# A two-layer decoder on one core: transposes moved ahead in each attention unit, maxima ahead of exponentials, probabilities scaled on ScalarE, every second low part of the weights made on GpSimd

## The chip, the cores and the metric

The kernel runs on one core of one Trainium2 chip, as one launch. The metric is the device time of that launch in microseconds (us). The kernel before took 1246.62 us as the median of three runs (1243.71 to 1250.85). The execution that the profile shows took 1248.97 us.

## The reference

Layer 1 is a RetNet layer (4 heads, chunks of 128) with a gate, an output projection and a gated embedding. Layer 2 is sparse attention with 16 heads in 4 groups over keys and values that the group shares. Everything is float32, 512 tokens by 1024.

```python
proj = rmsnorm(h, g_norm) @ w_in                     # layer 2
q, gate, bgate = jnp.split(proj, [q_w, q_w + NSA_W], axis=-1)
# per block of 128 queries:
p_c = softmax over the 31 compressed keys            # masked, causal
o_c = p_c @ v_cmp
idx = top_k(score, min(16, number of blocks))        # blocks of 64 keys
p_s = softmax over the keys of the selected blocks   # masked, causal
p_w = softmax over the last 512 keys                 # masked, causal
return gates[..., 0:1] * o_c + gates[..., 1:2] * o_s + gates[..., 2:3] * o_w
y = (silu(gate) * o) @ w_out
```

With 512 tokens there are 8 blocks, so all of them are selected, and the window of 512 reaches back to the first token. Both are plain causal attention, each with keys and values of its own. The compressed branch has 32 columns.

## The kernel before

**Arithmetic.** Every product is made from three: each operand is split into a high part (fp32r, a ScalarE copy) and a low part (the rest, a VectorE subtraction), and TensorE multiplies high by high, high by low and low by high (`mm3`). So each 128x512 result costs three passes for each 128 rows of depth.

**Weights.** `Stream` brings the weights in, 176 pieces of 128x1024 floats in a fixed order, through 4 raw buffers and 6 slots for the two parts. `mul` (line 176) multiplies a piece by its gain on GpSimd in two halves, `high` (line 190) copies it on ScalarE, `low` (line 205) subtracts on VectorE, and then `load` issues the DMA of a later piece into the raw buffer that became free (line 143, SP's queue). `tick(2)` does low, high, mul twice.

**The attention loop.** It goes through 4 groups `g` and in each through 8 units `u`: 4 heads, and of each the selected branch (`u` even, compressed columns with it) and the window branch (`u` odd). An iteration makes the scores of the next unit and the values of the current one, with projections in between that are independent (`fill(0)`, `fill(1)`, `fill(2)`; `PLAN` and `PARTS` say how many steps of 12 matmuls each has). In order:

- `scores(next)`: 15 matmuls into three banks tagged `s`; on VectorE the masks and the maxima (line 953), on ScalarE the exponentials into `P` (line 954). For the first two blocks of queries, which share a bank, a maximum and its exponential alternate. The compressed scores are added to their mask afterwards (line 893).
- `fill(0)`, then `scale_probs`: VectorE inverts the sums (962, 963), GpSimd multiplies `P` by them in four pieces (966).
- `fill(1)`, then `probs_split`: ScalarE copies the current unit's transposed probabilities `pt2` to `tH` (985), VectorE makes `tL` (986).
- `probs_T` for the next unit: VectorE transposes 32x32 blocks of `P` into `pt1` (975), four DMAs write them to DRAM (979), one brings them back in the other order into `pt2` (982).
- `W.tick(2)`, the sums of the compressed branch (900 to 903, and 904 on GpSimd), `cmp_T`, `fill(2)`, and `values(current)`: 12 matmuls from `tH` and `tL` into a bank tagged `o`.

The program runs in the order in which it is written, on each engine for itself; SP's queue as well issues its DMAs in that order and waits at each for what it needs. PSUM has eight banks: two `d`, three `s`, two `pt`, one `o`. Results of the projections in the loop go to `d`: a query or gate projection is two steps and one bank; a step of the output projection (`pair_tiles`) is two banks, and each is added to `hacc` on VectorE (1021). After the last unit of a group come the value projections of the next, and before it the key projections (`k_proj`), so the iterations u = 6 and 7 are long.

Of the kernel before, what the change touches and what calls it, by code (L numbers as in the profile page):

```python
# [11 lines left out]
F32 = mybir.dt.float32  # L12
# [3 lines left out]
OP = mybir.AluOpType  # L16
# [101 lines left out]
class Stream:  # L118
# [75 lines left out]
                self.nc.scalar.activation(hi[:, c], raw[:, c], AF.Copy, scale=g[:, k:k + 1])  # L194
        self.nh += 1

    def low(self):
        n = self.ns
        if n >= self.nh:
            return  # L200
        s = self.place[n]
        raw, m, w, g = self.parts(n)
        hi, lo = self.hi[s].bitcast(F32), self.lo[s]
        if g is None or w < 512:
            self.nc.vector.tensor_sub(lo[:, :m * w], raw, hi[:, :m * w])  # L205
        else:
            for k in range(m):
                c = slice(k * w, k * w + w)
                self.nc.vector.scalar_tensor_tensor(lo[:, c], raw[:, c], g[:, k:k + 1], hi[:, c],  # L209
                                                    op0=OP.mult, op1=OP.subtract)  # L210
        self.ns += 1
        self.load()
# [24 lines left out]
def decoder(ctx: ExitStack, tc: tile.TileContext, x, xT, stream, cst, msk, gains, fnorm, out):  # L237
# [32 lines left out]
    bg = V(fb + 508, 192).rearrange("p (t c) -> p t c", t=NT)  # L270
    fb += 700

    def psum(tag, shape=None):
        n = {"d": 2, "s": 3, "pt": 2, "o": 1}[tag]
        return ps.tile([128, 512], F32, name=tag, bufs=n)

# [198 lines left out]
    def run(g):  # L475
        for _ in g:
            pass
# [257 lines left out]

    def q_proj(g, h):
        p = W.get("nin", 0, 1024, 512 * g + 128 * h, 128)
        o = psum("d")
        wst(p, o, 0, 4)
        yield  # L740
        wst(p, o, 4, 8)
        s = 128 ** -0.5
        act.activation(q2H[h], o, AF.Copy, scale=s)
        dve.scalar_tensor_tensor(q2L[h], o, s, q2H[h].bitcast(F32), op0=OP.mult, op1=OP.subtract)
        W.tick()
        p.done()
        yield

    def g_proj(g, h):
        p = W.get("nin", 0, 1024, 2048 + 512 * g + 128 * h, 128)  # L750
        o = psum("d")
        wst(p, o, 0, 4)
        yield
        wst(p, o, 4, 8)
        x = g2[h % 2]
        act.activation(x, o, AF.Tanh, scale=0.5)
        dve.scalar_tensor_tensor(x, x, 1.0, o, op0=OP.add, op1=OP.mult)
        W.tick()
        p.done()
        yield  # L760
# [125 lines left out]
    PO = [0, 384, 768, 1152]  # L886
    JB = [0, 128, 224, 288]

    def cmp_probs(g, h, banks):

        q, q4 = pc[h % 2], pc4[h % 2]
        for i, o in banks:
            dve.tensor_add(q[:, i:i + 2], o, cmask[:, i:i + 2])
        mx, sm_ = scal(4), scal(4)
        dve.reduce_max(mx, q, axis=mybir.AxisListType.X)
        dve.tensor_sub(q, q, mx[:, :, None].to_broadcast([128, 4, 32]))
        yield
        act.activation(q, q, AF.Exp)
        yield
        dve.reduce_sum(sm_, q, axis=mybir.AxisListType.X)  # L900
        dve.reciprocal(sm_, sm_)
        dve.tensor_mul(sm_, sm_, bg[:, :, 12 * g + 3 * h])
        dve.tensor_mul(sm_, sm_, rowv)
        pool.tensor_mul(q4, q[:, :, None, :].to_broadcast([128, 4, 3, 32]),
                        sm_[:, :, None, None].to_broadcast([128, 4, 3, 32]))
        yield
# [11 lines left out]
    def scores(g, u):  # L918
        h, b = divmod(u, 2)
        e = 0 if b else 32  # L920
        mx, sm_ = scal(4), scal(4)
        cmp = []

        def block(w, i, lo, hi):
            c = slice(128 * i, 128 * i + 128)
            mm3(w, [(q2H[h][:, c], q2L[h][:, c], k2H[b][:, lo:hi], k2L[b][:, lo:hi])], True, True)

        for bank in ((3,), (2,), (0, 1)):
            o = psum("s")
            f, at = 0, []  # L930
            for i in bank:
                lo = e if i == 3 else 0
                n = 128 * i + 128 + e - lo
                block(o[:, f:f + n], i, lo, lo + n)
                at.append(f + e - lo)
                f += n
            if e and 2 in bank:
                block(o[:, 416:448], 3, 0, 32)
                cmp.append((2, o[:, 0:448].rearrange("p (a n) -> p a n", a=14)[:, 0:14:13]))
            elif e and 0 in bank:  # L940
                cmp.append((0, o[:, 0:480].rearrange("p (a n) -> p a n", a=3)[:, 0:2, :32]))
            if 1 in bank:

                d = bass.AP(tensor=o.tensor, offset=o.offset + e,
                            ap=[list(o.ap[0]), [256 + e, 2], [1, 128]])
                dve.tensor_add(d, d, tri[:, None, :].to_broadcast([128, 2, 128]))
            else:
                d = o[:, at[0] + 128 * bank[0]:][:, :128]
                dve.tensor_add(d, d, tri)
            for i, f in zip(bank, at):  # L950
                n = 128 * i + 128
                w = o[:, f:f + n]
                dve.reduce_max(mx[:, i:i + 1], w, axis=mybir.AxisListType.X, negate=True)  # L953
                act.activation(P[:, PO[i]:PO[i] + n], w, AF.Exp, bias=mx[:, i:i + 1],  # L954
                               accum_out=sm_[:, i:i + 1])
        chain = cmp_probs(g, h, cmp) if e else iter(())
        next(chain, 0)
        return sm_, chain

    def scale_probs(g, u, sm_):  # L960
        h, b = divmod(u, 2)
        dve.reciprocal(sm_, sm_)
        dve.tensor_mul(sm_, sm_, bg[:, :, 12 * g + 3 * h + b + 1])
        for i in (3, 2, 0, 1):
            w = P[:, PO[i]:PO[i] + 128 * i + 128]
            pool.tensor_scalar(w, w, sm_[:, i:i + 1], 1.0, op0=OP.mult, op1=OP.mult)  # L966

    def view(a, o, *ap):
        return bass.AP(tensor=a.tensor, offset=a.offset + o, ap=[list(a.ap[0])] + [list(d) for d in ap])

    def probs_T():


        for j in range(NT):
            dve.transpose(view(pt1, JB[j], (32, NT - j), (320, 4), (1, 32)),  # L975
                          view(P, PO[j] + 128 * j, (384, NT - j), (32, 4), (1, 32)))
        m = dr.tile([128, 1280], F32, name="moved")
        for a in range(4):
            nc.sync.dma_start(bass.AP(tensor=m.tensor, offset=m.offset + 320 * a,
                                      ap=[[1280, 32], [32 * 1280, 4], [1, 320]]),  # L980
                              pt1[32 * a:32 * a + 32].rearrange("p (b n) -> p b n", b=4))
        nc.sync.dma_start(pt2, m)

    def probs_split():
        act.activation(tH, pt2, AF.Copy)  # L985
        dve.tensor_sub(tL, pt2, tH.bitcast(F32))  # L986

    def values(g, u, o):
# [24 lines left out]
                yield  # L1013

    def pair_tile(c, t, p):
        o = psum("d")
        s = slice(128 * t, 128 * t + 128)
        mm3(o, [(y2H[:, k, s], y2L[:, k, s], p.h[:, k], p.l[:, k])
                for k in range(2)], True, True)
        d = hacc[:, t, 512 * c:512 * c + 512]  # L1020
        dve.tensor_add(d, d, o)  # L1021
# [10 lines left out]
    next(comp1)  # L1032
    w2p.done()
    probs_T()
    run(chain)
    k_proj(0, 1)

# [3 lines left out]
    for g in range(GROUPS):  # L1041
        f = fillers(g)
        for u in range(8):
            h = u // 2
            last = (g, u) == (3, 7)
            W.auto = False
            left = 2 * len(between(g, h))
            first = 4 if h == 3 else left // 2
            n = PLAN[u] if g == 3 else left - first if u % 2 else first
            steps = [1, 1, 0] if last else PARTS[n]  # L1050

            def fill(i):
                for _ in range(steps[i]):
                    next(f)

            sums = None
            if u < 7:
                nxt = g, u + 1
            elif g < 3:
                k_proj(g + 1, 0)  # L1060
                k_proj(g + 1, 1)
                nxt = g + 1, 0
            else:
                nxt = None
            if nxt:
                sums, chain = scores(*nxt)
            fill(0)
            if sums is not None:
                scale_probs(*nxt, sums)
            next(chain, 0)  # L1070
            fill(1)
            probs_split()
            if sums is not None:
                probs_T()
            W.tick(0 if last else 2)
            next(chain, 0)
            if u % 2 == 0:
                cmp_T(h)
            fill(2)
            if u % 2 == 0:  # L1080
                o_head = psum("o")
            values(g, u, o_head)
            W.auto = True
        run(f)
        if g < 3:
            p = v_pieces(g + 1)
            for t in range(NT):
                v_proj(g + 1, t, p, ("d", "pt")[t % 2], t % 2)
# [101 lines left out]
```

## Time and profile before

| what | before |
|---|---|
| time of the profiled execution | 1248.97 us |
| its span, first to last instruction | 1247.2 us |
| TensorE matmuls busy | 1146.7 us (92%) |
| VectorE busy | 753.4 us (60%) |
| ScalarE busy | 485.5 us (39%) |
| GpSimd busy | 324.9 us (26%) |
| mean granted TensorE clock | 0.96 |

The shares are means over stages that differ. Up to 586 us TensorE hardly stops; the attention loop from there to about 1180 us is where it waits. Matmuls are pipelined, so their busy time is not a measure of their speed. The granted clock is 1.00 at 2.4 GHz and 0.50 at 1.2 GHz; a mean between says how the stretch is shared between the two.

### The profile page before, as it was taken

The numbers are of one execution on the slowest core, as the hardware profiler recorded it, in microseconds if no ns is written. First come the engines' busy times: TensorE is split into PE (matmuls) and PEld (weight loads), VectorE is DVE, ScalarE is ACT, GpSimd is POOL, SyncE is SP. The second block draws the span as 40 slices with busy tenths as digits, with TensorE's granted clock in tenths as the row PEclk, the third lists the DMA queues.
The fourth block names the chain that finished last, engine by engine and source line by source line (L and its number), as shares of the span: only waits on it lengthen the run. The fifth ranks groups of instructions, "written<-read, shape, count | busy, mean of one in ns | idle before, by whom it ended". The sixth has DMA issues, their size and how long they took to land. (4 is left out here: it accounts for less than half of the span.)

```text
span 1247.2 us, 14924 instructions
## 1 busy us (share of the span) xinstructions
PE 1146.7 (92%) x5486; PEld 961.9 (77%) x5486; DVE 753.4 (60%) x1290; ACT 485.5 (39%) x852; POOL 324.9 (26%) x357
## 2 busy tenths in 40 slices
PE   9999999999999999997878898879988799878797
PEld 7888888888888888886767787768877688666686
DVE  4745446346435565566666656776576766777455
ACT  6432233233234554464333334442344323443454
POOL 0121012003002123556242304243134422221102
PEclk9999999999999999999788999999999899979899
DMA  8422322322322313454343333443424443353311
GB/s 326 138 73 85 105 85 85 101 93 68 105 81 68 115 39 124 155 161 135 99 150 119 110 118 115 152 135 106 138 83 146 135 135 110 107 170 124 99 51 68
DMA packets 52633, 143.84 MB, mean 115 GB/s; under 512 B 6096, under 2 KB 22736, under 8 KB 52560
## 3 DMA queue, kind: packets, MB, share of 16 engines
q1 hardware_dynamic: 52128, 142.10, 35.4%
q8 instruction: 43, 0.70, 0.2%
q10 hardware_dynamic: 432, 0.79, 0.2%
q14 instruction: 30, 0.25, 0.1%
HBM read 119.80 MB, written 23.07 MB: 115 GB/s over the span
## 5 line engine op out<-in xcount | busy, mean ns | idle before, releaser
L356 PE MATMUL d<-arenaR 128*128 128x512 f32 (+2 forms) x2904 | 686.2, 391 | 39.7 <-DVE arenaF L1021 27.2
L356 PEld LDWEIGHTS d<-arenaR 128*128 128x128 f32 x2904 | 538.4, 193 | 152.9 <-DVE arenaF L1021 32.3
L356 PE MATMUL s<-arenaR 128*128 128x512 f32 (+8 forms) x1182 | 249.1, 363 | 3.4 <-ACT arenaF L954 1.8
L356 PEld LDWEIGHTS s<-arenaR 128*128 128x128 f32 x1182 | 208.6, 197 | 35.1 <-ACT arenaF L954 2.0
L205 DVE TENSOR_TENSOR arenaR<-arenaF,arenaR 128x1024 fp32r<-128x1024 f32 (+1 forms) x142 | 179.6, 1282 | 67.0 <-ACT arenaR L190 66.8
L190 ACT ACTIVATE arenaR<-arenaF 128x1024 fp32r<-128x1024 f32 (+1 forms) x142 | 145.9, 1046 | 120.4 <-PE s L356 68.4
L356 PE MATMUL o<-arenaR 128*128 128x512 f32 (+3 forms) x744 | 148.5, 351 | 42.3 <-ACT arenaR L985 21.9
L356 PEld LDWEIGHTS o<-arenaR 128*128 128x128 f32 x744 | 126.3, 209 | 65.2 <-ACT arenaR L985 25.9
L176 POOL TENSOR_TENSOR arenaF<-arenaF 128x512 f32<-128x512 f32 x108 | 126.2, 1190 | 154.8 <-DMA arenaF<-stream_dram 150.4
L966 POOL TENSOR_SCALAR arenaF<-arenaF 128x512 f32<-128x512 f32 (+3 forms) x128 | 84.5, 678 | 231.2 <-ACT arenaR L985 79.8
L954 ACT ACTIVATE arenaF<-s,arenaF 128x512 f32<-128x512 f32 (+3 forms) x128 | 67.6, 528 | 134.4 <-DVE arenaF L953 132.3
L372 POOL TENSOR_TENSOR arenaF<-arenaF 128x1 f32<-128x1 f32 (+1 forms) x25 | 14.2, 568 | 292.3 <-DVE arenaF L371 292.3
L953 DVE TENSOR_REDUCE arenaF<-s 128x1 f32<-128x512 f32 (+3 forms) x128 | 62.8, 491 | 22.9 <-ACT arenaF L954 19.6
L356 PE MATMUL pt<-arenaR 128*128 128x512 f32 (+1 forms) x384 | 75.9, 349 | 0.0
L975 DVE STREAM_TRANSPOSE arenaF<-arenaF 128x512 f32<-128x512 f32 (+3 forms) x128 | 57.7, 489 | 25.0 <-POOL arenaF L966 23.9
L356 PEld LDWEIGHTS pt<-arenaR 128*128 128x128 f32 x384 | 62.8, 189 | 9.4
L209 DVE SCALAR_TENSOR_TENSOR arenaR<-arenaF,arenaR 128x512 fp32r<-128x512 f32 x64 | 45.7, 762 | 35.0 <-PE pt L356 21.4
L986 DVE TENSOR_TENSOR arenaR<-arenaF,arenaR 128x1280 fp32r<-128x1280 f32 x32 | 50.4, 1575 | 19.6 <-ACT arenaR L985 19.6
L194 ACT ACTIVATE arenaR<-arenaF 128x512 fp32r<-128x512 f32 x64 | 43.1, 720 | 46.5 <-issue 22.3
L1000 ACT ACTIVATE arenaR<-arenaF 128x512 fp32r<-128x512 f32 x16 | 10.1, 633 | 130.0 <-DVE arenaF L999 130.0
L1021 DVE TENSOR_TENSOR arenaF<-arenaF,d 128x512 f32<-128x512 f32 x64 | 42.0, 682 | 25.1 <-PE d L356 24.8
L985 ACT ACTIVATE arenaR<-arenaF 128x1280 fp32r<-128x1280 f32 x32 | 40.6, 1267 | 2.8 <-DMA arenaF<-moved 2.7
(125 smaller groups left out, 741.5 us busy)
## 6 DMA issues: line engine op xcount, KB each, us to landing
arenaF<-stream_dram SPq DMA_DIRECT2D x174, 512.0 KB, 4.2
moved<-arenaF SPq DMA_DIRECT2D x128, 160.0 KB, 2.8
arenaF<-moved SPq DMA_DIRECT2D x32, 640.0 KB, 4.0
arenaF<-xT_dram SPq DMA_DIRECT2D x8, 256.0 KB, 4.8
arenaF<-x_dram SPq DMA_DIRECT2D x4, 512.0 KB, 7.6
out_dram<-arenaF SPq DMA_DIRECT2D x3, 512.0 KB, 2.7
arenaF<-cst_dram SPq DMA_DIRECT2D x4, 256.0 KB, 3.9
arenaF<-stream_dram ACTq DMA_DIRECT2D x2, 256.0 KB, 3.4
```

What stands on the lines that cost most here:

```text
L176: self.nc.gpsimd.tensor_mul(r3[:, k], r3[:, k], g[:, k, None].to_broadcast([128, m // 2, w]))
L190: self.nc.scalar.activation(hi[:, :m * w], raw, AF.Copy)
L194: self.nc.scalar.activation(hi[:, c], raw[:, c], AF.Copy, scale=g[:, k:k + 1])
L205: self.nc.vector.tensor_sub(lo[:, :m * w], raw, hi[:, :m * w])
L209: self.nc.vector.scalar_tensor_tensor(lo[:, c], raw[:, c], g[:, k:k + 1], hi[:, c], op0=OP.mult, op1=OP.subtract)
L356: pe.matmul(o, a, b, start=start and i == 0, stop=stop and i == n - 1)
L953: dve.reduce_max(mx[:, i:i + 1], w, axis=mybir.AxisListType.X, negate=True)
L954: act.activation(P[:, PO[i]:PO[i] + n], w, AF.Exp, bias=mx[:, i:i + 1], accum_out=sm_[:, i:i + 1])
L966: pool.tensor_scalar(w, w, sm_[:, i:i + 1], 1.0, op0=OP.mult, op1=OP.mult)
L975: dve.transpose(view(pt1, JB[j], (32, NT - j), (320, 4), (1, 32)), view(P, PO[j] + 128 * j, (384, NT - j), (32, 4), (1, 32)))
L986: dve.tensor_sub(tL, pt2, tH.bitcast(F32))
L1021: dve.tensor_add(d, d, o)
```

## The change

Inside an iteration the current unit's split goes to the front, in two halves around the scaling; the scaling goes to ScalarE; the next unit's transposes and their four outgoing DMAs go ahead of `fill(1)`; the DMA back is issued just ahead of `values`. The weights' two rounds of low, high, mul are spread over the iteration, and the second low is made on GpSimd. Projections take a bank by the tag `f`, that is `d`, `pt`, `d` in turn.

```diff
-    def low(self):
+    def low(self, engine=None):
-            self.nc.vector.tensor_sub(lo[:, :m * w], raw, hi[:, :m * w])
+            (engine or self.nc.vector).tensor_sub(lo[:, :m * w], raw, hi[:, :m * w])
...
+    turn = [0]
     def psum(tag, shape=None):
+        if tag == "f":
+            turn[0] += 1
+            tag = ("d", "d", "pt")[turn[0] % 3]
...
-        o = psum("d")          # q_proj, g_proj, pair_tile
+        o = psum("f")
...
             for i, f in zip(bank, at):
+                dve.reduce_max(mx[:, i:i + 1], o[:, f:f + 128 * i + 128],
+                               axis=mybir.AxisListType.X, negate=True)
+            if cmp:
+                i, d = cmp
+                dve.tensor_add(pc[h % 2][:, i:i + 2], d, cmask[:, i:i + 2])
+            for i, f in zip(bank, at):
                 n = 128 * i + 128
-                w = o[:, f:f + n]
-                dve.reduce_max(mx[:, i:i + 1], w, axis=mybir.AxisListType.X, negate=True)
-                act.activation(P[:, PO[i]:PO[i] + n], w, AF.Exp, bias=mx[:, i:i + 1],
+                act.activation(P[:, PO[i]:PO[i] + n], o[:, f:f + n], AF.Exp, bias=mx[:, i:i + 1],
                                accum_out=sm_[:, i:i + 1])
...
-        for i in (3, 2, 0, 1):
+        for i in (3, 2, 1, 0):
             w = P[:, PO[i]:PO[i] + 128 * i + 128]
-            pool.tensor_scalar(w, w, sm_[:, i:i + 1], 1.0, op0=OP.mult, op1=OP.mult)
+            act.activation(w, w, AF.Copy, scale=sm_[:, i:i + 1])
...
     def probs_T():
-        for j in range(NT):
+        for j in (3, 2, 1, 0):
...
-        nc.sync.dma_start(pt2, m)
-    def probs_split():
+    def probs_back():
+        nc.sync.dma_start(pt2, moved.pop(0))
+    def probs_high():
         act.activation(tH, pt2, AF.Copy)
+    def probs_low():
         dve.tensor_sub(tL, pt2, tH.bitcast(F32))
...
                 sums, chain = scores(*nxt)
+            W.low()
             fill(0)
+            probs_high()
             if sums is not None:
                 scale_probs(*nxt, sums)
+            probs_low()
             next(chain, 0)
-            fill(1)
-            probs_split()
+            W.high()
+            W.mul()
             if sums is not None:
                 probs_T()
-            W.tick(0 if last else 2)
+            fill(1)
             next(chain, 0)
+            if not last:
+                W.low(nc.gpsimd)
+                W.high()
+                W.mul()
             if u % 2 == 0:
                 cmp_T(h)
             fill(2)
+            if sums is not None:
+                probs_back()
```

VectorE in iteration g = 1, u = 1, from the additions of `fill(0)` on, before: 1021 are additions to `hacc`, 962 and 963 invert the sums, 986 is `tL`, 975 the transposes, 205 the low parts, 900 to 903 the compressed sums.

```order
L1021 TENSOR_TENSOR arenaF<-arenaF,d 128x512 x2
L962 RECIPROCAL arenaF<-arenaF 128x4
L963 TENSOR_TENSOR arenaF<-arenaF 128x4
L1021 TENSOR_TENSOR arenaF<-arenaF,d 128x512 x2
L986 TENSOR_TENSOR arenaR<-arenaF,arenaR 128x1280
L975 STREAM_TRANSPOSE arenaF<-arenaF 128x4x4x32
L975 STREAM_TRANSPOSE arenaF<-arenaF 128x3x4x32
L975 STREAM_TRANSPOSE arenaF<-arenaF 128x2x4x32
L975 STREAM_TRANSPOSE arenaF<-arenaF 128x4x32
L205 TENSOR_TENSOR arenaR<-arenaF,arenaR 128x1024 x2
L900 TENSOR_REDUCE arenaF<-arenaF 128x4
```

The same place of the change (1035 are the additions, 970 and 971 invert the sums, 1000 is `tL`, 985 the transposes):

```order
L205 TENSOR_TENSOR arenaR<-arenaF,arenaR 128x1024
L1035 TENSOR_TENSOR arenaF<-arenaF,d 128x512 x2
L970 RECIPROCAL arenaF<-arenaF 128x4
L971 TENSOR_TENSOR arenaF<-arenaF 128x4
L1000 TENSOR_TENSOR arenaR<-arenaF,arenaR 128x1280
L985 STREAM_TRANSPOSE arenaF<-arenaF 128x4x32
L985 STREAM_TRANSPOSE arenaF<-arenaF 128x2x4x32
L985 STREAM_TRANSPOSE arenaF<-arenaF 128x3x4x32
L985 STREAM_TRANSPOSE arenaF<-arenaF 128x4x4x32
L1035 TENSOR_TENSOR arenaF<-arenaF,pt 128x512
L1035 TENSOR_TENSOR arenaF<-arenaF,d 128x512
L903 TENSOR_REDUCE arenaF<-arenaF 128x4
```

`tL` and the transposes now stand ahead of the additions of `fill(1)`; one low part stands ahead of the additions of `fill(0)`, and the other has left VectorE.

SP's queue in the iterations g = 1, u = 0 and 1, before (979 writes the transposed blocks, 982 brings them back, 143 loads weights):

```order
L979 DMA moved<-arenaF 32x4x320 x4
L982 DMA arenaF<-moved 128x1280
L143 DMA arenaF<-stream_dram 128x1024
L979 DMA moved<-arenaF 32x4x320 x4
L982 DMA arenaF<-moved 128x1280
L143 DMA arenaF<-stream_dram 128x1024 x2
```

The same iterations in the change (989 writes, 994 brings back):

```order
L989 DMA moved<-arenaF 32x4x320 x4
L143 DMA arenaF<-stream_dram 128x1024
L994 DMA arenaF<-moved 128x1280
L143 DMA arenaF<-stream_dram 128x1024
L989 DMA moved<-arenaF 32x4x320 x4
L143 DMA arenaF<-stream_dram 128x1024
L994 DMA arenaF<-moved 128x1280
```

A load that waits for a low part on GpSimd now stands between the writes and the DMA that brings them back.

ScalarE in iteration g = 1, u = 1, before (954 the exponentials, 898 that of the compressed branch, 985 `tH`, 190 high parts):

```order
L954 ACTIVATE arenaF<-s,arenaF 128x512
L954 ACTIVATE arenaF<-s,arenaF 128x384
L954 ACTIVATE arenaF<-s,arenaF 128x128
L954 ACTIVATE arenaF<-s,arenaF 128x256
L898 ACTIVATE arenaF<-arenaF 128x128
L985 ACTIVATE arenaR<-arenaF 128x1280
L190 ACTIVATE arenaR<-arenaF 128x1024 x2
```

And of the change (962 the exponentials, 997 `tH`, 974 the scaling, 901 the compressed branch):

```order
L962 ACTIVATE arenaF<-s,arenaF 128x512
L962 ACTIVATE arenaF<-s,arenaF 128x384
L962 ACTIVATE arenaF<-s,arenaF 128x128
L962 ACTIVATE arenaF<-s,arenaF 128x256
L997 ACTIVATE arenaR<-arenaF 128x1280
L974 ACTIVATE arenaF<-arenaF 128x512
L974 ACTIVATE arenaF<-arenaF 128x384
L974 ACTIVATE arenaF<-arenaF 128x256
L974 ACTIVATE arenaF<-arenaF 128x128
L901 ACTIVATE arenaF<-arenaF 128x128
L190 ACTIVATE arenaR<-arenaF 128x1024 x2
```

`tH` stays behind the exponentials, and the four scalings stand behind it.

## Rows read from the trace of the kernel before

**Rows 1.** Windows: bounds, length, busy us per engine (instructions), PEclk, DMA share, GB/s

```profile
0.00:586.50 586.50, 577.33 (x2759) 484.16 (x2759) 317.63 (x436) 229.16 (x340) 134.13 (x123) 1.00 0.34 114
603.70:699.10 95.40, 79.58 (x337) 65.87 (x338) 67.02 (x133) 36.86 (x76) 31.75 (x40) 0.86 0.40 126
749.80:849.60 99.80, 83.82 (x387) 69.22 (x387) 71.70 (x142) 39.15 (x80) 40.54 (x48) 0.93 0.39 121
902.90:1002.30 99.40, 84.33 (x387) 69.72 (x386) 72.84 (x143) 39.02 (x80) 41.16 (x47) 0.91 0.38 119
1002.30:1053.80 51.50, 48.36 (x275) 42.12 (x274) 30.27 (x60) 17.59 (x34) 10.18 (x14) 1.00 0.41 126
1053.80:1146.20 92.40, 74.93 (x339) 61.09 (x338) 68.52 (x139) 36.51 (x76) 23.94 (x33) 0.91 0.41 129
1146.20:1197.20 51.00, 43.67 (x200) 35.90 (x199) 29.69 (x54) 24.90 (x45) 6.18 (x8) 0.93 0.39 124
```

**Rows 2.** Windows of two single iterations, columns as in Rows 1

```profile
762.80:781.80 19.00, 14.90 (x67) 12.17 (x66) 14.40 (x30) 5.83 (x12) 2.92 (x5) 0.91 0.33 98
800.00:812.60 12.60, 12.60 (x66) 10.86 (x65) 7.65 (x17) 6.09 (x13) 2.81 (x4) 1.00 0.59 180
```

**Rows 3.** TensorE's waits: who for whom, us in total, times, longest us

```profile
PE d L356 <- DVE arenaF L1021: 27.2, 16, 3.4
PE o L356 <- ACT arenaR L985: 21.9, 11, 3.0
PE o L356 <- DVE arenaR L986: 13.2, 12, 1.6
PE d L356 <- DVE arenaF L757: 11.9, 4, 4.8
PE pt L912 <- POOL arenaF L904: 6.2, 2, 3.1
```

**Rows 4.** Timeline 1109 to 1124 us: start, us, instruction, idle before and its end

```profile
1109.15 1.27 ACT L985 ACTIVATE arenaR<-arenaF 128x1280 fp32r<-128x1280 f32 x1
1110.45 1.50 DVE L986 TENSOR_TENSOR arenaR<-arenaF,arenaR 128x1280 fp32r<-128x1280 f32 x1 [1.42 <-ACT arenaR L985]
1112.59 1.84 DVE L975 STREAM_TRANSPOSE arenaF<-arenaF 128x512 f32<-128x512 f32 x4 [0.64 <-POOL arenaF L966]
1114.46 1.88 SPq L979 DMA_DIRECT2D moved<-arenaF  x4
1115.46 0.27 DVE L900 TENSOR_REDUCE arenaF<-arenaF 128x4 f32<-128x128 f32 x1
...
1116.52 0.83 POOL L904 TENSOR_TENSOR arenaF<-arenaF 128x384 f32<-128x384 f32 x1 [3.96 <-DVE arenaF L903]
...
1118.84 0.34 SPq L982 DMA_DIRECT2D arenaF<-moved  x1
...
1123.12 1.27 ACT L985 ACTIVATE arenaR<-arenaF 128x1280 fp32r<-128x1280 f32 x1 [0.21 <-DMA arenaF<-moved]
```

**Rows 5.** Groups by line: xcount, busy us, mean ns of one, idle before and releasers

```profile
L966 POOL TENSOR_SCALAR arenaF<-arenaF 128x512 f32<-128x512 f32 (+3 forms) x128 | 84.5, 678 | 231.2 <-ACT arenaR L985 79.8 <-ACT arenaF L898 67.5 <-DVE arenaF L963 43.7
L954 ACT ACTIVATE arenaF<-s,arenaF 128x512 f32<-128x512 f32 (+3 forms) x128 | 67.6, 528 | 134.4 <-DVE arenaF L953 132.3 <-PE s L356 0.6 <-PE d L356 0.3
L953 DVE TENSOR_REDUCE arenaF<-s 128x1 f32<-128x512 f32 (+3 forms) x128 | 62.8, 491 | 22.9 <-ACT arenaF L954 19.6
L1021 DVE TENSOR_TENSOR arenaF<-arenaF,d 128x512 f32<-128x512 f32 x64 | 42.0, 682 | 25.1 <-PE d L356 24.8
```

**Rows 6.** Single lines: xcount, shortest, median and longest ns, first and last start

```profile
L176 POOL TENSOR_TENSOR arenaF<-arenaF x108: 1030/1040/2289, 439.8 to 1067.9; 128x512 f32<-128x512 f32 x108
L205 DVE TENSOR_TENSOR arenaR<-arenaF,arenaR x142: 679/1218/2062, 14.3 to 1160.2; 128x1024 fp32r<-128x1024 f32 x138, 128x912 fp32r<-128x912 f32 x2, 128x608 fp32r<-128x608 f32 x1, 128x512 fp32r<-128x512 f32 x1
L428 POOL TENSOR_TENSOR arenaF<-arenaF x8: 1278/1289/2200, 35.7 to 307.7; 128x512 f32<-128x512 f32 x8
```

**Rows 7.** DMA issues: xcount, KB each, median us from issue to landing

```profile
arenaF<-stream_dram SPq DMA_DIRECT2D x174, 512.0 KB, 4.2
```

More of the change, by code (lines that the diff above doesn't have):

```diff
@@ L750, in g_proj @@
         p = W.get("nin", 0, 1024, 2048 + 512 * g + 128 * h, 128)
-        o = psum("d")
+        o = psum("f")
         wst(p, o, 0, 4)
@@ L887, in decoder, with cmp_probs @@
     JB = [0, 128, 224, 288]
-    def cmp_probs(g, h, banks):
+    def cmp_probs(g, h):
         q, q4 = pc[h % 2], pc4[h % 2]
-        for i, o in banks:
-            dve.tensor_add(q[:, i:i + 2], o, cmask[:, i:i + 2])
         mx, sm_ = scal(4), scal(4)
@@ L921, in scores @@
         mx, sm_ = scal(4), scal(4)
-        cmp = []
         def block(w, i, lo, hi):
@@ L938, in scores @@
                 block(o[:, 416:448], 3, 0, 32)
-                cmp.append((2, o[:, 0:448].rearrange("p (a n) -> p a n", a=14)[:, 0:14:13]))
+                cmp = 2, o[:, 0:448].rearrange("p (a n) -> p a n", a=14)[:, 0:14:13]
             elif e and 0 in bank:
-                cmp.append((0, o[:, 0:480].rearrange("p (a n) -> p a n", a=3)[:, 0:2, :32]))
+                cmp = 0, o[:, 0:480].rearrange("p (a n) -> p a n", a=3)[:, 0:2, :32]
+            else:
+                cmp = None
             if 1 in bank:
@@ L950, in scores @@
             for i, f in zip(bank, at):
+                dve.reduce_max(mx[:, i:i + 1], o[:, f:f + 128 * i + 128],
[4 more added lines that the diff above has]
+            for i, f in zip(bank, at):
                 n = 128 * i + 128
-                w = o[:, f:f + n]
-                dve.reduce_max(mx[:, i:i + 1], w, axis=mybir.AxisListType.X, negate=True)
-                act.activation(P[:, PO[i]:PO[i] + n], w, AF.Exp, bias=mx[:, i:i + 1],
+                act.activation(P[:, PO[i]:PO[i] + n], o[:, f:f + n], AF.Exp, bias=mx[:, i:i + 1],
                                accum_out=sm_[:, i:i + 1])
-        chain = cmp_probs(g, h, cmp) if e else iter(())
+        chain = cmp_probs(g, h) if e else iter(())
         next(chain, 0)
@@ L963, in scale_probs @@
         dve.tensor_mul(sm_, sm_, bg[:, :, 12 * g + 3 * h + b + 1])
-        for i in (3, 2, 0, 1):
+        for i in (3, 2, 1, 0):
             w = P[:, PO[i]:PO[i] + 128 * i + 128]
-            pool.tensor_scalar(w, w, sm_[:, i:i + 1], 1.0, op0=OP.mult, op1=OP.mult)
+            act.activation(w, w, AF.Copy, scale=sm_[:, i:i + 1])
     def view(a, o, *ap):
         return bass.AP(tensor=a.tensor, offset=a.offset + o, ap=[list(a.ap[0])] + [list(d) for d in ap])
+    moved = {}
     def probs_T():
-        for j in range(NT):
+        for j in (3, 2, 1, 0):
             dve.transpose(view(pt1, JB[j], (32, NT - j), (320, 4), (1, 32)),
                           view(P, PO[j] + 128 * j, (384, NT - j), (32, 4), (1, 32)))
-        m = dr.tile([128, 1280], F32, name="moved")
+        m = moved[0] = dr.tile([128, 1280], F32, name="moved")
         for a in range(4):
@@ L1015, in pair_tile @@
     def pair_tile(c, t, p):
-        o = psum("d")
+        o = psum("f")
         s = slice(128 * t, 128 * t + 128)
@@ L1079, in decoder @@
             fill(2)
+            if sums is not None:
+                probs_back()
             if u % 2 == 0:
```

## The prediction

> **What bounds the kernel now.** I read the windows first. Up to 586.5 us TensorE is busy for 577.3 of 586.5 us at a clock of 1.00 [rows 1]: nothing is to be had there, and the change hardly touches it. In the attention loop each of the four stretches of six short units (603.7 to 699.1, 749.8 to 849.6, 902.9 to 1002.3, 1053.8 to 1146.2) has TensorE idle for 15 to 17 us, at a clock of 0.86 to 0.93, so part of it is at 1.2 GHz [rows 1]. Two iterations with the same matmuls show the size: one without a wait takes 12.6 us at clock 1.00, one with waits 19.0 us at 0.91 [rows 2]. No engine is full: VectorE has 67 to 73 us in 92 to 100.
>
> The waits, read second, have three kinds [rows 3]: for a `d` bank that VectorE has not added or gated yet (1021, 757: 39.1 us), for `tH` and `tL` in `values` (985, 986: 35.1 us), for the compressed probabilities from GpSimd (904: 6.2 us). They are waits for order rather than for work. `tH` stands on ScalarE behind the evacuation of `fill(1)`, and the additions stand on VectorE behind the whole softmax.
>
> Third, the timeline of one unit shows the loop underneath [rows 4]: `tH` at 1109.15 (1.27), `tL` at 1110.45 (1.50), transposes at 1112.59 (1.84), first write at 1114.46, the way back issued at 1118.84, next `tH` at 1123.12, released by that DMA. That is 13.97 us from `tH` to `tH`; without the 0.64 that the transposes wait for GpSimd's scaling it is 13.3. Each link follows from the one before, in the changed order too: `tL` precedes the next transposes on VectorE, and the next `tH` needs their DMA. So 13.3 us is a floor for a unit, above the 12.6 us that TensorE needs for the longest of the short ones, and against (95.4 + 99.8 + 99.4 + 92.4) / 24 = 16.1 us that they take.
>
> **The change part by part.** *Split ahead of `fill(1)`.* `tH` now waits for the exponentials and its DMA alone. The 35.1 us go as far as the floor allows; what is late next is the round trip.
>
> *Bank tag `f`.* Three or four results can be open instead of two. In a unit with six output tiles TensorE then stops perhaps once, for a tile whose addition stands behind the maxima and one low part; I cost that at nothing, since the floor covers it. The 39.1 us go. If that cover fails it is the second rival.
>
> *Scaling on ScalarE.* GpSimd loses 128 instructions, 84.5 us [rows 5]. ScalarE gains 128. It shows no float32 copy of `P` with a scale there; the nearest rows are the exponentials of the same four shapes, mean 0.528, 2.1 us a unit, and GpSimd's own, 0.678, 2.7 us. Below nothing is excluded, as they are new work on ScalarE. I take 2.1, the same engine. They run beside `tL` and the first transposes, whose order (smallest matrix last needed first) follows the scaling's; 1.50 of `tL` plus the transposes hide them, and the 0.64 of GpSimd's scaling is gone. Were they 2.7, 0 to 0.6 would show.
>
> *Maxima first.* The 19.6 us that maxima waited for exponentials [rows 5] go, 0.6 a unit. They lie ahead of `tH`, where the round trip has slack, so I count nothing; the range has 0 to 0.6 a unit in it.
>
> *Low parts.* There are 26 on GpSimd. A low part of 1024 there has no row; 512 of two full inputs took 1.289 (428), so two would be 2.58; the gain in 512 took 1.040 (176), two 2.08 [rows 6]. Below 2.08 I exclude, as it reads a second full input; above I take two of the longest of 176, 4.6. I choose 2.45, near 428, less one start. VectorE is spared 26 of 1.22, but it is not the bound.
>
> *SP's queue.* The DMA back was issued when the writes had landed; now a weight load precedes it, and that load waits for GpSimd's low part. Behind it on SP stand the way back and everything later; `tH`, and so `values`, waits for them. In odd units GpSimd first makes the compressed probabilities, whose sums now follow two additions on VectorE: 2 x 0.68 + 1.06 (1115.46 to 1116.52) + 0.83 + 2.45, about 5.7 us after the transposes, against 4.4 in the timeline (1114.46 to 1118.84): 1.2 later. Then the way back shares the DMA engines with a load of 512 KB just ahead, 4.2 us when it lands as usual [rows 7]; I take 1.0 for that, bounds 0 and 4.2. In even units the low part ends while the writes are under way; I take 0.5 for their delay by the load, bounds 0 and 1.4. And a gain on GpSimd can hold up `tL`: 176 has a median of 1.040 and a longest of 2.289 us, 205 on VectorE 1.218 and 2.062 [rows 6], so now and then one stretches by about the length of the other. That is 0 to 1.04 us for `tL`; I take 0.4 (0.2 where no low part runs on GpSimd).
>
> The Trainium skill (SBUF — State Buffer, SBUF: two separate sides) has this as a rule: a VectorE instruction with two SBUF inputs and a GpSimd instruction that reads SBUF exclude each other for their whole length. The trace agrees with it by the stretched lengths just named. It speaks against moving low parts to GpSimd, since one of them would hold VectorE more than twice as long as half a gain does; what that makes of the time is the third rival, which is worked out from rows.
>
> **The sum.** The 24 short units are 10 even ones with a low part on GpSimd at 13.3 + 0.4 + 0.5 = 14.2, 9 odd ones at 13.3 + 1.2 + 1.0 + 0.4 = 15.9, and 5 without at 13.5: 142.0 + 143.1 + 67.5 = 352.6. After a long pair the first unit has a head start of about 1.8 (12.6 of TensorE's work; its `tL` is ready earlier than `values`), three times: 347.2, against 387.0, a gain of 39.8. Each of the three long pairs (51.5 us and two like it) holds one wait for `tH` and `tL` of 2.65; two thirds go, 5.0 in all. In the last 51.0 us stretch two such waits stand; I take 3.0, bounds 0 and 8. Together 47.8: 1249.0 - 47.8 = 1201.2 us for the profiled execution. That one lay 2.4 above the median of the runs, so 1199 us.
>
> **Rivals.** *The bare round trip.* GpSimd's low parts and the loads fall beside the writes after all, and units run at 13.3: 24 x 13.3 - 5.4 = 313.8, a gain of 73.2, with 5.0 and 5.0: 1249.0 - 83.2 - 2.4 = 1163 us. For it: GpSimd is idle over half of each stretch [rows 1]. Against: on SP the load stands ahead of the way back whatever GpSimd does.
>
> *The banks still stop TensorE.* VectorE now has `tL` and the transposes, 3.3 us, ahead of the additions of `fill(1)`, and a low part ahead of those of `fill(0)`. Seven short units have six tiles; each then keeps its 19.0 instead of 15.9: 7 x 3.1 = 21.7 more, 1221 us. Against: the third and fourth bank.
>
> *The low part on the round trip: slower.* If a low part on GpSimd holds VectorE for its whole length, one of 2.45 ahead of `tL` or of the sums costs it whole, and it waits itself up to 2.29 - 1.04 = 1.25 for VectorE: 3.7 us in each of the 19 units, 70 us: 1199 + 70 = 1269 us. It decides from 2.5 us a unit (47.8 / 19), that is when the way back leaves some 12 us after `tH`, instead of the 9.7 in the timeline. Against: by the written order low parts start after the transposes, when `tL` is over, so only small products of VectorE are in the way.
>
> That the change does not do what it says is ruled out by the order of the instructions.
>
> **How the numbers follow.** Forecast 0.50, bare round trip 0.17, banks 0.19, low part on the round trip 0.14, the last with all costs between nothing and 70. A measurement of this kernel tells about 0.5% from no change. The forecast, the bare round trip and the banks are faster (0.86); of the last, 0.06 lie within 0.5% and 0.08 above. The range from 1164 to 1228 holds the forecast with its bounds, most of the banks and half of the bare round trip, about 0.8. Likeliest: 1199.
>
> **What would show it.** In the profile of the changed kernel TensorE's waits for 985 and 1021 should be small, and what remains should be a wait in `values` for `tH` that ends with the DMA from `moved`. `tH` to `tH` should be 13.5 to 16 us in short units, the way back should be issued later after the transposes in odd units than in even ones, directly behind a load. The low parts on GpSimd should take 2.3 to 2.6 us and the four scalings 2.1. I am wrong if units run at 12.6 to 13.3 with no wait, if `tL` often starts when a GpSimd low part ends, or if TensorE's largest wait is still for a bank.

## The result, and the profile after

The changed kernel takes 1190.26 us (median of 4 runs, 1187.62 to 1193.80), against 1248.73 us for the kernel before (4 runs): a ratio of 0.9536, 95% interval 0.949 to 0.9581. The forecast was 1199.

The first part of the page says how busy each engine was over the whole span of 1192.0 us:

```profile
PE 1127.1 (95%) x5486; PEld 949.4 (80%) x5486; DVE 733.7 (62%) x1264; ACT 540.5 (45%) x980; POOL 305.1 (26%) x255
```

TensorE does the same 5486 matmuls in 1127.1 us, where the table ahead has 1146.7, with a mean clock of 0.971 after 0.96. The scalings have moved from GpSimd to ScalarE. The windows answer to [rows 1]: four stretches of short units, one long pair, the last stretch.

```profile
605.10:683.50 78.40, 71.27 (x336) 59.74 (x337) 62.97 (x133) 46.76 (x100) 20.34 (x17) 0.93 0.53 155
731.30:819.60 88.30, 81.56 (x386) 68.13 (x385) 68.50 (x141) 48.28 (x102) 34.87 (x27) 0.94 0.48 144
867.30:954.80 87.50, 79.29 (x387) 65.75 (x386) 70.02 (x142) 48.28 (x102) 36.31 (x28) 0.98 0.51 149
954.80:1002.50 47.70, 47.70 (x275) 42.05 (x273) 28.17 (x52) 22.48 (x44) 15.02 (x12) 1.00 0.40 123
1002.50:1089.80 87.30, 72.25 (x338) 60.58 (x337) 63.37 (x139) 45.38 (x98) 16.41 (x11) 0.90 0.48 138
1089.80:1142.00 52.20, 43.11 (x199) 35.17 (x198) 26.69 (x46) 26.47 (x49) 4.50 (x4) 0.90 0.34 109
```

The span is 55.2 us shorter: the short units take 78.4 + 88.3 + 87.5 + 87.3 = 341.5 instead of 387.0, so 45.5; the three long pairs 143.2 instead of 155.5, so 12.3, and in the one shown TensorE is busy for all of 47.70 us, at clock 1.00; the last stretch 52.2 instead of 51.0, 1.2 lost; and the loop begins 1.4 later.

What TensorE waits for in the loop answers to [rows 3]:

```profile
PE o L361 <- ACT arenaR L997: 18.9, 7, 6.1
PE d L361 <- DVE arenaF L1035: 13.0, 5, 5.6
PE o L361 <- DVE arenaR L1000: 11.9, 15, 1.0
```

Line 997 makes `tH`, 1000 `tL`, 1035 adds an output tile (985, 986 and 1021 before). The waits for a `d` bank are down from 39.1 us to 13.0, the gates' share (757 before, 762 now) to none, that for GpSimd's compressed probabilities to none. `tH` is still waited for nearly as long in all (18.9 us after 21.9), but 7 times instead of 11.

One odd unit of group 1 shows the new loop, as [rows 4] showed the old one; 985 are transposes, 989 the writes, 994 the way back, 143 a weight load, 907 and 205 GpSimd's compressed probabilities and low part:

```profile
754.60 1.91 DVE L985 STREAM_TRANSPOSE arenaF<-arenaF 128x128 f32<-128x128 f32 x4
...
756.53 1.88 SPq L989 DMA_DIRECT2D moved<-arenaF  x4
...
758.62 0.83 POOL L907 TENSOR_TENSOR arenaF<-arenaF 128x384 f32<-128x384 f32 x1 [15.04 <-DVE arenaF L906]
...
759.40 2.40 POOL L205 TENSOR_TENSOR arenaR<-arenaF,arenaR 128x1024 fp32r<-128x1024 f32 x1
...
761.83 0.35 SPq L143 DMA_DIRECT2D arenaF<-stream_dram  x1
762.41 0.34 SPq L994 DMA_DIRECT2D arenaF<-moved  x1
...
768.43 1.27 ACT L997 ACTIVATE arenaR<-arenaF 128x1280 fp32r<-128x1280 f32 x1 [2.35 <-DMA arenaF<-moved]
```

The last write had landed at 760.78, so the way back was free to go then. It stood on SP behind a load into the raw buffer that GpSimd's low part (759.40 to 761.80) still had to read, left at 762.41, and landed 5.9 us later, with the 512 KB just issued ahead of it.

The groups by line that answer to [rows 5]; then the way back's landing times, shortest, median and longest, over 32:

```profile
L205 POOL TENSOR_TENSOR arenaR<-arenaF,arenaR 128x1024 fp32r<-128x1024 f32 x26 | 62.4, 2399 | 92.4 <-ACT arenaR L190 92.4
L974 ACT ACTIVATE arenaF<-arenaF 128x512 f32<-128x512 f32 (+3 forms) x128 | 61.1, 549 | 1.8 <-DVE arenaF L971 1.8
L997 ACT ACTIVATE arenaR<-arenaF 128x1280 fp32r<-128x1280 f32 x32 | 40.7, 1272 | 46.4 <-DMA arenaF<-moved 44.6 <-PE d L361 1.7
L955 DVE TENSOR_REDUCE arenaF<-s 128x1 f32<-128x512 f32 (+3 forms) x128 | 59.9, 489 | 3.3
```

```profile
DMA to landing us min/median/max: 3.8/4.5/7.0
```

A low part on GpSimd takes 2.40 us, four scalings on ScalarE 4 x 0.549 = 2.2, the maxima hardly wait. Of the 46.4 us that ScalarE stands idle before `tH`, 44.6 end with the DMA.

### The profile page after: what moved, and what is told of

Same layout as the page of the kernel before. It is cut to its first block, busy times and chain, and to the rows that moved or that the text cites. A ratio compares the mean times of both kernels' runs of the same rounds, so it can differ in the third digit from the quotient of the medians.

```text
span 1192.0 us, 14867 instructions
## 1 busy us (share of the span) xinstructions
PE 1127.1 (95%) x5486; PEld 949.4 (80%) x5486; DVE 733.7 (62%) x1264; ACT 540.5 (45%) x980; POOL 305.1 (26%) x255
## 5 line engine op out<-in xcount | busy, mean ns | idle before, releaser
L361 PE MATMUL d<-arenaR 128*128 128x512 f32 (+2 forms) x2568 | 597.5, 387 | 14.6 <-DVE arenaF L1035 13.0
L361 PEld LDWEIGHTS d<-arenaR 128*128 128x128 f32 x2568 | 469.0, 190 | 109.0 <-DVE arenaF L1035 16.2
L205 DVE TENSOR_TENSOR arenaR<-arenaF,arenaR 128x1024 fp32r<-128x1024 f32 (+2 forms) x116 | 151.5, 1319 | 65.7 <-ACT arenaR L190 65.4
L361 PE MATMUL o<-arenaR 128*128 128x512 f32 (+3 forms) x744 | 144.1, 343 | 36.1 <-ACT arenaR L997 18.9
L361 PE MATMUL pt<-arenaR 128*128 128x512 f32 (+1 forms) x720 | 158.4, 369 | 1.6 <-DVE arenaR L371 1.4
L176 POOL TENSOR_TENSOR arenaF<-arenaF 128x512 f32<-128x512 f32 x108 | 130.5, 1230 | 85.3 <-DMA arenaF<-stream_dram 81.0
L361 PEld LDWEIGHTS pt<-arenaR 128*128 128x128 f32 x720 | 125.6, 189 | 24.4 <-DVE arenaR L371 1.7
L377 POOL TENSOR_TENSOR arenaF<-arenaF 128x1 f32<-128x1 f32 (+1 forms) x25 | 14.2, 570 | 294.4 <-DVE arenaF L376 294.4
L205 POOL TENSOR_TENSOR arenaR<-arenaF,arenaR 128x1024 fp32r<-128x1024 f32 x26 | 62.4, 2399 | 92.4 <-ACT arenaR L190 92.4
L1000 DVE TENSOR_TENSOR arenaR<-arenaF,arenaR 128x1280 fp32r<-128x1280 f32 x32 | 47.8, 1493 | 51.6 <-ACT arenaR L997 51.6
L907 POOL TENSOR_TENSOR arenaF<-arenaF 128x384 f32<-128x384 f32 x16 | 13.3, 829 | 224.8 <-DVE arenaF L906 210.3
L194 ACT ACTIVATE arenaR<-arenaF 128x512 fp32r<-128x512 f32 x64 | 43.1, 720 | 46.5 <-issue 22.3
L974 ACT ACTIVATE arenaF<-arenaF 128x512 f32<-128x512 f32 (+3 forms) x128 | 61.1, 549 | 1.8 <-DVE arenaF L971 1.8
L997 ACT ACTIVATE arenaR<-arenaF 128x1280 fp32r<-128x1280 f32 x32 | 40.7, 1272 | 46.4 <-DMA arenaF<-moved 44.6
L985 DVE STREAM_TRANSPOSE arenaF<-arenaF 128x128 f32<-128x128 f32 (+3 forms) x128 | 57.7, 489 | 3.7 <-ACT arenaR L190 0.5
```

Source lines behind the costliest of these rows:

```text
L176: self.nc.gpsimd.tensor_mul(r3[:, k], r3[:, k], g[:, k, None].to_broadcast([128, m // 2, w]))
L205: (engine or self.nc.vector).tensor_sub(lo[:, :m * w], raw, hi[:, :m * w])
L361: pe.matmul(o, a, b, start=start and i == 0, stop=stop and i == n - 1)
L974: act.activation(w, w, AF.Copy, scale=sm_[:, i:i + 1])
```

## The experiments

Ratios are to the kernel before, run beside each on the same chip (medians there 1248.7 to 1251.9 us, so differences of a few us between runs are better read from the ratios); line numbers in the rows are those of the changed kernel unless said. "Changed" stands for the changed kernel.

**1. Way back directly behind its writes.**

```diff
             if sums is not None:
                 probs_T()
+                probs_back()
             fill(1)
 ...
             fill(2)
-            if sums is not None:
-                probs_back()
```

> The changed kernel with one edit: the DMA that brings the transposed probabilities back is issued directly behind the four writes, ahead of the weight load that waits for the second low part. Round trip theory (the changed kernel's short units are held by the way from one tH to the next, and the load ahead of the way back lengthens it): the way back leaves 0.1 to 0.2 us after the last write has landed and lands after 3.9 us instead of 4.5 to 7; tH to tH is 13.0 to 13.4 in short units, which take about 318 us instead of 341.5; time about 1168 us against 1190 of the changed kernel. Rival, banks: what holds the units are additions on VectorE ahead of which TensorE finds no bank; then 1185 to 1190. Rival, GpSimd's low parts hold VectorE: no difference, 1190.

1174.59 us, ratio 0.9404 (0.9379 to 0.9428): 16 us less than changed, where 22 were expected. The way back's landing times and TensorE's waits:

```profile
DMA to landing us min/median/max: 3.8/3.9/4.5
```

```profile
PE o L361 <- ACT arenaR L997: 10.7, 6, 3.7
PE o L361 <- DVE arenaR L1000: 10.3, 12, 1.6
PE d L361 <- DVE arenaF L1035: 8.9, 6, 4.1
```

It now leaves at most 0.5 us after its last write has landed, lands in 3.8 to 4.5 us, and the short units take 324.6 instead of 341.5. The wait for banks shrinks too, though no bank was touched. So its place on SP's queue behind a load cost 16 us.

**2. GpSimd's low parts back on VectorE**: `W.low(nc.gpsimd)` becomes `W.low()`.

> The changed kernel with the second low part on VectorE again. Round trip theory: the load behind it is issued about 1.1 us sooner in nine odd units (2.40 on GpSimd against 1.3), and VectorE has 1.2 us more in each of 26 places where it mostly has room: 1183 to 1196, no clear change. Rival, GpSimd's low parts hold VectorE's two-input instructions: clearly faster, 1170 to 1180. Rival, VectorE is the bound of the units with six tiles: slower by 26 x 1.2 = 31, about 1220.

1190.47 us, 0.9528 (0.9509 to 0.9547): no difference. Its waits show two effects against each other:

```profile
PE d L361 <- DVE arenaF L1035: 15.4, 8, 4.7
PE o L361 <- ACT arenaR L997: 14.3, 7, 4.7
```

The way back in the nine odd short units with such a low part now leaves 0.05 to 0.4 us after its last write, not 0.5 to 1.9, so `tH` is waited for less (14.3 for 18.9); the additions, with 26 low parts more ahead of them on VectorE, are waited for more (15.4 for 13.0). The short units take 340.1 us, against 341.5. Nearly half of what the earlier departure gives is lost again in the landing, since the load still goes just ahead of the way back, which lands in 5.1 us on average in those nine units instead of 4.7. From the end of the transposes to the landing these units gain 0.7 us; with experiment 1, which puts the load behind the way back, they gain 2.0. The landing times of all 32 here:

```profile
DMA to landing us min/median/max: 3.8/5.2/5.6
```

**3. The old banks in the new order.**

```diff
         if tag == "f":
             turn[0] += 1
-            tag = ("d", "d", "pt")[turn[0] % 3]
+            tag = "d"
```

> The changed kernel with the projections in the loop on the two banks d alone again. Round trip theory: the floor covers part of the bank waits; the seven units with six tiles go back to about 19 us, so 15 to 25 us slower, 1205 to 1215. If the banks carry all that they waited before (39.1 us): 1229. If the round trip covers them wholly: 1190 to 1194.

1211.96 us, 0.9703 (0.9681 to 0.9725): 22 us more than changed, in the range given. The waits for a `d` bank are back:

```profile
PE d L361 <- DVE arenaF L1035: 22.8, 15, 4.3
PE d L361 <- DVE arenaF L762: 18.6, 7, 6.3
```

**4. Scaling on GpSimd, in the new order**: line 974 becomes `pool.tensor_scalar(w, w, sm_[:, i:i + 1], 1.0, op0=OP.mult, op1=OP.mult)`.

> The changed kernel with the four scalings on GpSimd again. Round trip theory: the scaling stands behind a gain or a low part on GpSimd and the transposes wait for it, 0.6 to 2 us in each of 24 short units: 1204 to 1230. If the scaling is covered wherever it stands: 1190. If ScalarE was burdened by it (61 us more busy): faster, about 1180.

1189.87 us, 0.953 (0.9505 to 0.9555): no difference, so the first theory's 1204 to 1230 is a miss. A scaling there takes 0.696 us instead of 0.549, but the transposes' waits grow only from 3.7 to 8.9 us over 128 of them: with `tL` between, the scaling is covered on either engine.

**5. The round trip cut out of the loop.** On top of 1, the way back reads the block that the unit before wrote, from a third DRAM buffer. So it leaves out the wait for the four writes, and each unit's values are made with the probabilities of the unit before: it tells a time and cannot be used.

```diff
-        nc.sync.dma_start(pt2, moved.pop(0))
+        nc.sync.dma_start(pt2, moved.pop(0) if len(moved) > 1 else moved[0])
```

> The kernel of x1_back_early, but the DMA back reads what the unit before wrote (a third DRAM buffer), so it need not wait for the four writes just issued; same instructions and bytes, and the attention weights used in a unit are those of the unit before. Round trip theory: the trip from tH to tH loses the 2.9 us of the writes' landing and falls to about 10, below the 12.5 that TensorE needs; tH's waits for its DMA go, the short units take 300 to 312 us instead of 324.6, time 1150 to 1162 against 1174.6 of x1_back_early. Rival, banks and VectorE's order hold the units: 1170 to 1175.

1161.96 us, 0.9309 (0.9281 to 0.9338). That is the upper edge of what was expected. The short units take 313.4 us, 13.1 each, a little over the 300 to 312. So 12.6 of the 28.3 us between changed and this one are the round trip's that 1 still has; the other 15.7 went with 1.

**6. The way back twice**, on top of 1: `nc.sync.dma_start(pt2, m)` stands two times.

> The kernel of x1_back_early with the DMA back issued twice from the same buffer. Round trip theory: every short unit's trip grows by the second transfer, 1.3 to 2 us, 21 units bound by it: 27 to 42 us, 1200 to 1217. Rival, the trip has slack and the units are held by something else: 1175 to 1180.

1255.96 us, 1.006 (1.004 to 1.008): 81 us more than 1, about twice the most expected. SP's waits say why (995 and 996 are the two):

```profile
SPq L996 <- DMA arenaF<-moved: 113.5, 32, 4.0
```

Both write `pt2`, so in this program the second was issued only when the first had landed, 3.5 us later on average in each of 32 units; the first theory had counted it beside the first. That a unit pays for a longer trip is shown.

**7. The banks alone, in the old order**: tag `f` added to the kernel before, nothing else.

> The kernel before with the tag f alone. Bank waits of 39.1 us go, and with them their stretches at 1.2 GHz, but the units end at the old order's waits for tH and tL, and part of the time goes there: 1215 to 1230 by the round trip theory (floor 13.3 and the old split behind fill(1)). If the two kinds of wait are independent: 1200 to 1208. If the old order eats it all: 1245.

1235.57 us, 0.9899 (0.9869 to 0.9929): 13 us less, where 19 to 34 were expected. Its waits (990 and 991 are `tH` and `tL` there):

```profile
PE o L361 <- ACT arenaR L990: 34.6, 15, 4.9
PE o L361 <- DVE arenaR L991: 16.9, 16, 1.8
PE d L361 <- DVE arenaF L1026: 11.8, 7, 3.0
PE pt L917 <- POOL arenaF L909: 9.6, 2, 4.9
```

The waits for banks fell from 39.1 to 11.8, and those for `tH`, `tL` and GpSimd rose from 41.3 to 61.1. All but the banks is -37 us (experiment 3, which holds the order, the maxima first and the two changes of engine), banks alone -13, both -58. The 8 us by which both are more than the sum are barely clear of the runs' intervals; where the banks' waits went when they came alone, the rows show.

**8. Transposes ahead of `tL`**, on top of 1: `scale_probs`, `probs_T`, then `probs_high`, `probs_low`, `probs_back`.

> The kernel of x1_back_early with scaling, transposes and writes of the next unit ahead of tH and tL of the current one. Round trip theory: the transposes no longer follow tL, so the trip is no loop any more except through pt2; tH stands 2 us later in its unit, tL behind the transposes, and values in units of two steps wait for it, but six-tile and three-step units run at 12.6 to 13.2: short units 312 to 322, time 1162 to 1172. If tL behind the transposes costs more than the loop did: 1175 to 1190.

1211.55 us, 0.9714 (0.9673 to 0.9755): a miss, 37 us more than 1. The trip begins earlier, but `values` waits in nearly every unit:

```profile
PE o L361 <- DVE arenaR L1000: 25.7, 29, 1.0
PE o L361 <- ACT arenaR L997: 24.9, 16, 3.8
```

`tH` and `tL` now stand behind the next unit's softmax, which needs the next unit's scores; those stand on TensorE behind `values` of the unit before. By the order of the instructions the loop runs through scores, maxima, scaling, transposes, `tL` and `values`; short units take 14.6 us on average.

**9. Two-bank ring**, on top of 1: `("d", "pt")[turn[0] % 2]`.

> The kernel of x1_back_early with the tag f as d, pt, d, pt instead of d, pt, d, so that a bank d comes again after four results and not after three. In three units (1,5), (2,5) and (3,5) of x1_back_early the fourth tile waits 1 to 4 us for a bank d although the low part and the additions ahead are all that stand there. Banks theory for the rest: these waits go, 3 to 8 us, 1166 to 1172. Round trip theory alone: no change, 1173 to 1176. Rival, pt is now short for the compressed transposes and value projections: slower, 1178 to 1190.

1183.25 us, 0.946 (0.9434 to 0.9487): slower than 1 and in the rival's range, but not by its cause: no compressed transpose and no value projection stands among the long waits. One line tells it:

```profile
PE pt L361 <- DVE arenaF L762: 17.7, 6, 4.3
```

Line 762 is a gate projection's last step on VectorE; before each of these six waits it ran directly behind `tL` and the four transposes. While it waits, its `pt` bank is taken.

**10. First low part behind `fill(0)`**, on top of 1.

```diff
             if nxt:
                 sums, chain = scores(*nxt)
-            W.low()
             fill(0)
+            W.low()
```

> The kernel of x1_back_early with the first low part behind the additions of fill(0) instead of ahead. The banks of fill(0) come free 1.2 us sooner; what stands ahead of the inverted sums is as long as before. Banks theory: 3 to 6 us less, 1168 to 1172; round trip theory: no change, 1173 to 1176.

1171.83 us, 0.9361 (0.9339 to 0.9382), short units 322.9, waits for 1035 of 6.2 instead of 8.9 us: as expected, if barely apart from 1.

**11. 9 and 10 together.**

> Both edits, of x9_ring and x10_low_later. Banks theory: 1163 to 1170. Round trip theory: 1173 to 1176.

1185.79 us, 0.9473 (0.9446 to 0.95): a miss. The ring's loss stays whole, as it is the gate's.

**12. The ring, with the gate always in a `d` bank**: 9, and `o = psum("d")` in `g_proj`.

> The way back early and the bank ring (d, pt) of x9, but the gate projection always in a d bank, so that only the output tiles alternate. Theory that the loss of x9 (1183 against 1175 us) is the gate's pt bank, held until VectorE is past the low part and the transposes: TensorE's waits for line 762 (17.7 us) go, the units that now take 14.5 to 19.9 come to 12.6 to 14, and the time is 1162 to 1172 us, at or under the best so far (1171.8). Rival that the gate's bank blocks wherever it stands: a d bank held equally long stops the output tiles of fill(1) and fill(2) instead, waits for 762 or 1035 of 12 us or more remain, and the time is 1176 to 1188 us.

1167.96 us, 0.9357 (0.9331 to 0.9383), 15 us less than 9 (13 by the ratios), as the theory had it. No wait for a bank stands among the first:

```profile
PE o L361 <- ACT arenaR L997: 12.8, 6, 2.9
PE o L361 <- DVE arenaR L1000: 12.6, 16, 1.3
PE o L361 <- DVE arenaR L801: 4.2, 5, 1.6
```

With 10 it is the best version, by ratio the same as that: both beat the changed kernel by 1.8 to 1.9% and lie some 0.5% above experiment 5, which has no round trip in its loop.

## Why the prediction was right, point by point

**The loop.** Right: the wait that is left in `values` ends with the DMA from `moved`, and experiments 1, 5 and 6 move the time by moving that trip alone. From `tH` to `tH` it took 12.8 to 13.3 us in the five short units where no load stood ahead; the floor said 13.3.

**SP's queue.** Right in kind; in size right for odd units and too small for even ones. In the forecast's own three classes, the time from the end of the transposes to the landing is 8.3 us on average in the five units without a low part on GpSimd, 10.3 in the nine odd ones and 9.7 in the ten even ones: +2.0 where 1.2 + 1.0 were forecast, and +1.4 where 0.5 was. (The 1.2 should have been 1.3 by its own terms, 5.7 less 4.4.) In odd units the way back leaves 1.3 us later and takes 0.7 us longer to land. In even units the load ahead costs the writes 0.4 us, as forecast, but the way back another 1.0: it leaves 0.02 to 0.15 us after the last write and lands in 5.0 us on average instead of 4.0. I had charged that load to the writes alone.

**`tL` held up by GpSimd, 0.4 a unit**: nothing. All 32 `tL` took 1.49 us. By these errors against each other the classes come out close: from `tH` to `tH` 14.4 us on average in even units (14.2 forecast), 15.5 in odd ones (15.9), 13.0 in the five without (13.5).

**The sum of the short units**: 347.2 forecast, 341.5 measured, again by two errors against each other, so that it is this close is partly luck. The two units behind a long pair take 25.6, 26.3 and 25.6 us where 14.2 + 15.9 - 1.8 = 28.3 were set down: the probabilities of the first landed 5.7 to 7.9 us before its `tH`, so by these prices the head start is not 1.8 but 3.8 to 4.5. The first stretch is 78.4 instead of 84.1 (14.2 + 4 x 13.5 + 15.9). That is 13.1 less. The other twelve take 185.6 instead of 178.2.

**Long pairs**: 12.3 gained, not 5.0. I let two thirds of one wait of 2.65 go; all waits went, 9.2 us of idle TensorE with two short waits for a bank, since the data of the second unit had landed 8 us or more before `tH` and `tH` no longer stands behind `fill(1)`. The other 3.1 are TensorE's work itself, 2.2 of them in the second pair, whose clock was 0.97 and is now 1.00. **Last stretch**: -1.2 instead of +3.0, with a wait for `tH` of 6.1 us; the way back ahead of it left on time and took 6.3 us to land behind a load. Experiment 1 has 49.1 there. These two terms were the worst sized; together they are 11.1 where 8.0 were forecast. The loop also begins 1.4 us later, which the forecast had not. In all 55.2 us of span went where 47.8 were forecast.

**The banks at nothing.** In the changed kernel 13.0 us of bank waits remain, at most 5.6 at a time, and the longest of them is the round trip's, passed on:

```profile
1074.01 0.34 SPq L994 DMA_DIRECT2D arenaF<-moved  x1
...
1079.31 1.27 ACT L997 ACTIVATE arenaR<-arenaF 128x1280 fp32r<-128x1280 f32 x1 [3.69 <-DMA arenaF<-moved]
1080.49 1.91 ACT L974 ACTIVATE arenaF<-arenaF 128x512 f32<-128x512 f32 x4
1080.62 1.49 DVE L1000 TENSOR_TENSOR arenaR<-arenaF,arenaR 128x1280 fp32r<-128x1280 f32 x1 [3.89 <-ACT arenaR L997]
1082.02 1.91 DVE L985 STREAM_TRANSPOSE arenaF<-arenaF 128x128 f32<-128x128 f32 x4
...
1083.86 1.25 DVE L1035 TENSOR_TENSOR arenaF<-arenaF,d 128x512 f32<-128x512 f32 x2
...
1084.56 2.93 PE L361 MATMUL d<-arenaR 128*128 128x512 f32 x6 [5.62 <-DVE arenaF L1035]
```

TensorE waits for an addition; the addition stands behind the transposes and `tL`; `tL` behind `tH`; `tH` behind the DMA. That DMA left 0.08 us after its last write and took 5.3 us to land, with a load issued 2.2 us ahead. Read as a bank wait it asks for more banks, read down the engine it asks for a DMA that lands sooner, and experiment 1 took 4.1 us off the whole kind by that alone (10 leaves 6.2 of it and 12 next to none, each for 0.5% more). So the cover held in the main, though not at nothing. TensorE's largest wait in sum is the one for `tH`, as forecast; its longest single ones are close, 6.1 us for `tH` and 5.6 for a bank.

**Low parts and scaling.** 2.40 us against 2.45 chosen, 2.2 against 2.1. The later way back that the forecast put on GpSimd's low part in odd units is there (0.5 to 1.9 us after the last write) and goes without it (experiment 2), but so does what VectorE is spared, which the forecast had at nothing. Which engine scales does not matter (experiment 4). So these two parts bring nothing by themselves; what the maxima ahead of the exponentials bring was not run alone. The Trainium skill (SBUF — State Buffer, SBUF: two separate sides) has it that a VectorE instruction with two inputs in SBUF and a GpSimd one that reads SBUF exclude each other. Single lengths agree, as a gain here has a median of 1.042 and a longest of 2.389 us, but in the sum of experiment 2 nothing of it shows. Three lines tell why (1015 makes the low part of the gated result, 1001 before; 1000 is `tL`):

```profile
L1001 DVE TENSOR_TENSOR arenaR<-arenaF,arenaR x16: 691/692/693, 639.4 to 1176.1; 128x512 fp32r<-128x512 f32 x16
L1015 DVE TENSOR_TENSOR arenaR<-arenaF,arenaR x16: 693/1382/2589, 632.7 to 1118.7; 128x512 fp32r<-128x512 f32 x16
L1000 DVE TENSOR_TENSOR arenaR<-arenaF,arenaR x32: 1490/1493/1494, 613.0 to 1112.3; 128x1280 fp32r<-128x1280 f32 x32
```

Ten of the 26 low parts on GpSimd ran beside line 1015, which has two inputs in SBUF. It then took 1.37 to 2.59 us and ended 0.54 to 0.55 us after the low part each time; the additions beside the same low parts, which read a bank, kept their 0.68. So a low part on GpSimd does hold VectorE, but what it met here is one short instruction off the trip, for which no engine waited, and never `tL`.

**The rivals.** Units at the bare trip (1163) needed the way back first in the queue, which the change had not done; experiment 1 goes 16 of the 27 us. Banks as the bound (1221) is what experiment 3 comes near to (1212). The low part on the trip (1269) is refuted by experiment 2 and by the length of `tL`.

## What to carry to other kernels

In a loop whose length is a trip through DRAM, issue the DMA of that trip ahead of the other loads in its queue: here two lines moved gave 16 us, more than the banks alone (13). A wait for a buffer behind an in-order engine is to be followed down that engine to its first late input before buffers are added; and where buffers are added, what holds one longest (here the gate) gets one of its own kind.

## What the runs showed of the hardware that was not expected

The 640 KB way back landed in 3.8 to 4.5 us where it was issued right behind its writes (experiment 1), and in up to 7.0 us in the changed kernel, where in 26 of 32 units a 512 KB load had gone just ahead of it on the same queue; in the other six it took 3.8 to 4.2. And in this program a second DMA to the same destination was not work beside the first: in experiment 6 the queue stood 113.5 us in 32 waits. A subtraction of two inputs in SBUF on VectorE, 0.69 us by itself, took up to 2.59 us beside a low part on GpSimd, and ended after it.
